# Scores contracted over 128 rows: key parts laid out twice, or padded with zeros

## The chip, the cores and the metric

The kernel runs on one core of a Trainium2 chip. The metric is device time in microseconds (us), the median of several runs. TensorE (PE in the profile) multiplies; its weight loads have a row of their own (PEld). VectorE (DVE), ScalarE (ACT) and GpSimd (POOL) do the rest of the arithmetic, and SyncE (SP) issues most DMAs.

## What is computed

One sequence of 512 tokens with 1024 features goes through two hybrid layers and then one layer of a second kind. Everything is float32. The parts that matter here are the score products; cut to those, the reference is:

```python
# hybrid layer (twice): 6 heads of 64, over 8 chunks of 64 tokens
scores = einsum('bnqhd,bnkhd->bnhqk', q * HEAD_DIM ** -0.5, kb)   # chunk attention, causal by chunk
p = softmax(where(valid, scores + bias, NEG_INF));  o = einsum('bnhqk,bnkhd->bnqhd', p, vb)
q, k = rotary(q), rotary(k) * HEAD_DIM ** -0.5                    # retention
y = (decayed q.k scores within and across chunks) @ v, layer norm, times silu(g)
mix = concat([y_att, y_conv, y_ret]) @ w_out ; then a squared-relu MLP 1024 -> 4096 -> 1024
# second kind: feed-forward, then state space model + dilated attention + attention over a memory, feed-forward
# dilated attention: 3 patterns x 4 heads of 64, windows (128, stride 1), (512, 4), (2048, 16)
```

Every score has a head's 64 dimensions as its contraction.

## The kernel before, in words

Activations lie feature-major: a tile `t` has 128 features in its partitions and the 512 tokens in its columns. So a tile of queries or keys holds two heads, one in rows 0 to 63 and one in rows 64 to 127.

Products keep float32's accuracy by splitting each operand into a high part in TensorE's faster float32r format (by ScalarE, `split`) and the low part that remains (by VectorE, `lo`); three products of parts, high by high, low by high and high by low, are summed in PSUM (`mm3`). All linear layers (`gemm`) do so: weights come by SP as `raw`, are split into `wh` and `wl`, and each 512-token product has 128 rows and 128 columns of weights. They make up nearly all of TensorE's work.

Nothing runs in the order in which it is written. `Plan` records the whole program; `order` then simulates the five engines with a cost for each operation (`_cost`; a matmul's cost there goes by its columns and not by how many rows it contracts) and takes the ready operation of least priority number; `emit` writes the instructions in that order. The order is fixed at build time: each engine, and SP's queue of DMAs, works strictly down its list. `ahead` and `filler` shift priorities. Work beside the linear layers (convolution, attention, retention, state space model) is written as generators that `gemm` steps between its products (`pump_all`, `pump`). All tiles of activations come from one pool of 80 slots (`T`), PSUM has 8 banks (`psa`, `psg`), and weights in flight have 3 `raw` and 4 each of `wh` and `wl`.

The scores:

- Chunk attention and retention (6 heads each, in both hybrid layers) lay the queries of a pair of heads out with `stack`, so that one tile has the high part of a head over its low part, in all 128 rows; `twice` lays the high part of the keys out in both halves. Per block of 128 queries (or keys) there are two products: `mm(qs, kd)` over 128 rows gives high by high plus low by high, and `mm(qs[rows], kl[rows])` over 64 rows gives high by low. Block sizes are 128, 256, 384 and 512 columns. Per layer this is 6 x 4 blocks for each of the two, 96 blocks in both layers. ScalarE and VectorE then read the bank; in retention POOL masks the diagonal (`affine_select`).
- Dilated attention of stride 1 (`dilated_near`, 4 heads x 4 blocks) uses `scores`: three products over 64 rows.
- Dilated attention of strides 4 and 16 (`dilated_far`, 4 heads x 4 residues x 2 patterns) takes plain float32 with one instruction over 64 rows, which the profile counts as two.

`stack` and `twice` move halves between partitions with `move`, a DMA on SP of 64 x 512 elements. The third move of a tile overwrites what the first two have read.

Of the kernel before, what the change touches and what calls it, by code (L numbers as in the profile page):

```python
# [120 lines left out]
def _dilated_bias(table):  # L121
    """per head [128, 256] for the pattern of stride 1 (key block before | same block) and
    [128, 256] for the patterns of strides 4 | 16 within the tokens of one residue modulo 4"""
    t = np.asarray(table, np.float32).reshape(32, 3, DH)
    q = np.arange(P)[:, None]
    k = np.arange(2 * P)[None, :]
    o = q + P - k
    b0 = np.where(((o >= 0) & (o <= P))[..., None], t[_buckets(np.clip(o, 0, P)), 0], np.float32(NEG))
    o = q - np.arange(P)[None, :]
    d = _buckets(4 * np.maximum(o, 0))  # L130
    b1 = np.where((o >= 0)[..., None], t[d, 1], np.float32(NEG))
    b2 = np.where(((o >= 0) & (o % 4 == 0))[..., None], t[d, 2], np.float32(NEG))
    out = np.stack([b0, np.concatenate([b1, b2], axis=1)])
    return np.ascontiguousarray(out.transpose(3, 0, 1, 2), np.float32)


def _pairs(a):
    """[32 groups, 64 states, ...] -> [128 (group % 2, state), 16, ...]"""
    a = np.asarray(a)
    return np.ascontiguousarray(np.moveaxis(a.reshape(PAIRS, 2 * STATE, *a.shape[2:]), 0, 1))  # L140
# [48 lines left out]
class _Engine:  # L189
    """stands for an engine of nc while the program is recorded"""  # L190
# [10 lines left out]
class Plan:  # L201
    """Records the program, orders it by a model of the engines' times (a list scheduler: the ready
    operation of the least priority number goes first) and emits it in that order. An operation that
    takes a slot of a pool ahead of its turn does so only where the operations in between still find
    theirs."""
# [12 lines left out]
    def ahead(self, n):  # L218
        """the operations within count as recorded n operations before"""
        return _Ahead(self, n, False)  # L220

    def filler(self, n):
        """the operations within count as recorded n operations later, and fill gaps before"""
        return _Ahead(self, -n, True)
# [22 lines left out]
    def record(self, eng, fn, method, args, kw):  # L247
# [19 lines left out]
        for w, aps in ((False, reads), (True, writes)):  # L267
            for ap in aps:
# [15 lines left out]
                if n in self.tiles:  # L284
                    t = self.tiles[n]
                    if isinstance(t, str):
                        self.tiles[n] = t = [t, op, op]
                    t[2] = op
                    a = self.acc.setdefault(n, [])
                    if a and a[-1] is not op:  # L290
                        # what opens a tile goes first, and products into a bank keep their order:
                        # the start of one clears the marks of what the others have written there
                        op.deps.add(a[-1] if w and eng == "PE" else t[1])
                    if not a or a[-1] is not op:
                        a.append(op)
# [44 lines left out]
    def order(self):  # L340
# [39 lines left out]
        while len(out) < len(ops):  # L380
# [49 lines left out]
            else:  # L430
# [4 lines left out]
                if e == "PE":  # L435
                    # the clock is halved after a tick of little work
                    tick = int(s / self.TICK)
                    if work.get(tick - 1, 0.0) < 3060:
                        c *= 2
                    work[tick] = work.get(tick, 0.0) + o.cols  # L440
# [53 lines left out]
class Net:  # L494
# [66 lines left out]
    def lo(self, src, hi, out=None):  # L561
        """src - hi as the low part"""
# [12 lines left out]
    def stack(self, src):  # L575
        """parts of two heads -> the high part over the low part of the first, and the low over the high
        part of the second"""
# [8 lines left out]
    def twice(self, src):  # L586
        """parts of two heads -> the high part of each in both halves; the low parts"""
        h, l = src
        o = self.T(F32R)
        lo, hi = slice(0, HD), slice(HD, P)  # L590
        self.move(o[hi], h[hi])
        self.move(o[lo], h[hi])
        self.move(h[hi], h[lo])
        return h, o, l

    def wload(self, src, n=KT * P):
        """one unit of weights, split"""
# [16 lines left out]
    def pump_all(self, bg):  # L614
        """of each [generator, n] in bg n steps"""
# [23 lines left out]
    def gemm(self, srcs, acts, evict, wide=4, bg=None, steps=0, per=1, both=False):  # L639
        """for each source of weights `per` psum tiles [128, S]; the contraction runs outermost  # L640
        over the first `wide` of them"""
# [25 lines left out]
    def rsqrt(self, v, n):  # L667
        """1 / sqrt(v), one step of Newton behind the square root of the table"""
# [10 lines left out]
    def colsum(self, ps, i, m, tile_, rhs, w=1, n=NB):  # L679
        """adds tile_^T rhs to ps[128 tokens, n * w], tile i of m"""  # L680
# [5 lines left out]
    def bcast(self, r, ps=None, n=NB):  # L686
        """r [128 tokens, n] -> psum [128, n * 128], the same in every row"""
# [6 lines left out]
    def bcast2(self, r2):  # L694
        """r2 [128 tokens, NB * 2] -> psum [128, S], rows 0-63 from the first, 64-127 from the second"""
# [14 lines left out]
    def rms_r(self, tiles, n=D, out=True):  # L710
        """1 / rms per token, broadcast to [128, S] in SBUF, or PSUM"""
# [27 lines left out]
    def hsplit(self, x, gname):  # L739
        """x * g per feature, split; the factor per token comes behind the product"""  # L740
        return [self.hsplit1(t, self.col(gname, k)) for k, t in enumerate(x)]

    def post(self, f, gname, nname):
        """x += rms_norm(f) * g; the new x for the norm that follows, as by hsplit"""
# [10 lines left out]
    def vtok(self, vt, b):  # L755
        """tiles [128 features, S] -> psum [128 tokens of block b, heads, 64]"""
# [5 lines left out]
    def vsplit(self, blocks):  # L762
        """token-major values of the blocks of keys, [128 tokens, heads, 64] each -> for block j and
        head h the high part beside the low part, v(j, h) [128, 2, 64]"""
# [21 lines left out]
    def av1(self, v, o, ph, pl, start, stop):  # L786
        """o[0:64] + o[64:128] += v^T probs"""
# [13 lines left out]
    def chunk_attention(self, l, q, k, v, mix):  # L801
        nc = self.nc
        mm = nc.tensor.matmul
        vt = self.vsplit(self.vtok(v, b) for b in range(NB))
        yield
        for h in range(HEADS):
            rows = slice((h % 2) * HD, (h % 2) * HD + HD)
            qs, kd, kl = q[h // 2][h % 2], k[h // 2][h % 2], k[h // 2][2]
# [7 lines left out]
            for b in range(NB):  # L816
# [3 lines left out]
                mm(ps[:, :n], qs[:, c], kd[:, :n], start=True, stop=False)  # L820
                mm(ps[:, :n], qs[rows, c], kl[rows, :n], start=False, stop=True)
# [27 lines left out]
    def fold(self, po, out):  # L849
        """rows 0-63 plus rows 64-127"""  # L850
# [36 lines left out]
    def rotate(self, ps, cr, sr):  # L887
        """the halves of each head trade places by way of DMA"""
# [23 lines left out]
    def retention(self, q, k, v, g, mix):  # L912
        nc = self.nc
        mm = nc.tensor.matmul
        for h in range(HEADS):
            rows = slice((h % 2) * HD, (h % 2) * HD + HD)
            qs, kd, kl = q[h // 2][h % 2], k[h // 2][h % 2], k[h // 2][2]
# [3 lines left out]
            for j in range(NB):  # L921
# [3 lines left out]
                mm(ps[:, :n], kd[:, c], qs[:, j * P:], start=True, stop=False)  # L925
                mm(ps[:, :n], kl[rows, c], qs[rows, j * P:], start=False, stop=True)
# [150 lines left out]
    def exp(self, x, n):  # L1077
        """e^x in place on [128, n], to float32's accuracy"""
# [20 lines left out]
    def cmul(self, ore, oim, are, aim, bre, bim, t, u):  # L1099
        """(ore, oim) = a b; t, u: room"""  # L1100
# [8 lines left out]
    def ssm_prepare(self):  # L1109
        """what depends on the state space model's parameters alone. A chunk of 8 tokens, rows  # L1110
        (7 - token, input) of a group: kernel within the chunk, map to the states at its end, map
        from the states before it, and the states' rotation over the chunks"""
# [183 lines left out]
    def ssm_start(self, tiles):  # L1296
        """tiles of u [128 features, (token of the chunk, chunk)] -> DRAM"""
# [6 lines left out]
    def halves(self, src):  # L1304
        """[P, 1024] of DRAM as two tiles"""
# [5 lines left out]
    def ssm(self, out):  # L1311
        """few columns a product: float32 as it is costs less than its parts"""
# [81 lines left out]
    def softmax_rows(self, s, ps, bias, m, l):  # L1394
        """s = exp(ps + bias - max), the maximum to m, the sum to l"""
# [18 lines left out]
    def vkeep(self, blocks):  # L1414
        """token-major values of the blocks, v(j, h) [128, 64]"""
# [12 lines left out]
    def dilated_near(self, q, k, v, stat, ys):  # L1428
        """stride 1: keys 0 to 128 back"""
# [4 lines left out]
        for h in range(DH):  # L1434
            rows = slice((h % 2) * HD, (h % 2) * HD + HD)
            qq, kk = q[h // 2], k[h // 2]
# [5 lines left out]
            for blocks in ((1, 2), (0, 3)):  # L1442
                ps, s = self.psa(), T()
                c = 0
                for b in blocks:
                    n = 2 * P if b else P
                    self.scores(ps[:, c:c + n], qq, slice(b * P, (b + 1) * P), kk,
                                slice((b + 1) * P - n, (b + 1) * P), rows)
# [29 lines left out]
    def dilated_far(self, q, k, v, stat, ys):  # L1478
        """strides 4 and 16, within the tokens of one residue modulo 4; float32 as it is"""
# [4 lines left out]
        for h in range(DH):  # L1484
# [6 lines left out]
            for r2 in range(2):  # L1491
                ps, s = self.psa(), T(F32, (P, 2, 2, P))
                pv = ps.rearrange("p (r i c) -> p r i c", r=2, i=2)
                for j in range(2):
                    c = slice((r2 * 2 + j) * P, (r2 * 2 + j + 1) * P)
                    for i in range(2):
                        mm(pv[:, j, i], q[i][h // 2][rows, c], k[i][h // 2][rows, c], start=True, stop=True,
                           skip_group_check=True)
# [20 lines left out]
    def dilated_join(self, near, far, y0, y1, out):  # L1519
        """the two parts' sums, each with its own maximum, as one softmax"""  # L1520
# [35 lines left out]
    def memory_start(self):  # L1556
        """the memory, normed but for the factor per token, split"""
# [43 lines left out]
    def memory(self, u):  # L1601
        """keys (u < 4) or values of a head -> DRAM: [128 dims, memory], values [128 memory, dims]"""
# [95 lines left out]
    def tail(self, srcs, acts, out):  # L1698
        """the last products, and behind them the last norm, by halves of the tokens"""
# [73 lines left out]
    def mixer2(self):  # L1773
# [28 lines left out]
        def qkv(pattern, st):  # L1802
            def e(i, ps):
# [10 lines left out]
                st[kind].append(t if kind == 0 or pattern else self.split(t))  # L1814
# [118 lines left out]
```

## Time and profile before

| | |
|---|---|
| three runs | 2509.88, 2514.57 and 2519.38 us, median 2514.57 us |
| profiled execution | span 2510.5 us, 30038 instructions; no further time of its own is given |
| PE busy | 2483.7 us, 99% of the span, 11522 matmuls |
| PEld busy | 2033.4 us (81%) |
| DVE busy | 1462.8 us (58%) |
| ACT busy | 946.0 us (38%) |
| POOL busy | 110.7 us (4%) |
| mean granted TensorE clock | 0.989 of full speed |

The span runs from the first to the last instruction of the profiled execution. Busy time is the union of an engine's instructions; matmuls overlap one another and their ends are modelled, so a busy PE may still be slow. Since every recorded operation is issued from the one line in `emit`, all rows say L475, and they are told apart by their tiles (`t`, `p` for PSUM, `wh`, `wl`) and by their form: `64*128 64x512` is a product over 64 rows with 128 weight columns and 512 columns of output, `128*128 128x512` one over 128 rows. An entry x2 on the timeline is two neighbours of one line and one pair of tiles, merged; the form shown is that of the first. The hybrid layers' mixers lie at about 20 to 230 us and 640 to 870 us, the second kind's mixer at about 1690 to 2030 us.

### The profile page before, as it was taken

To read this page: it belongs to the slowest core of one execution; us is meant where nothing else is said; L and a number is where in the kernel's file an instruction comes from. 1 tells how busy PE (TensorE), PEld (TensorE's weight loads), DVE (VectorE), ACT (ScalarE), POOL (GpSimd) and SP (SyncE) were. 2 spreads that over 40 slices of the span, in tenths; PEclk is the share of its full clock that TensorE was granted. 3 is DMA by queue.
4 is the path that set the end of the run, shared out by engine and by line. 5 is a ranking of instruction groups with operands and counts; after the bars stand their busy time and mean duration, and the time that the engine had idled before them with its cause. 6 is when DMAs were issued, how large, how long until landed. Compare 5 with 4: busy or idle time off the path is not lost.

```text
span 2510.5 us, 30038 instructions
## 1 busy us (share of the span) xinstructions
PE 2483.7 (99%) x11522; PEld 2033.4 (81%) x11522; DVE 1462.8 (58%) x2529; ACT 946.0 (38%) x1482; POOL 110.7 (4%) x214
## 2 busy tenths in 40 slices
PE   8999999999999999999999999999999999999998
PEld 7777888888887788788888888888878888888887
DVE  7985734545897579934565444456445555444445
ACT  4465532223346453322343222234455433322222
POOL 0011000000001100310000000000000000000000
PEclk9998999999999899999999999999999999999999
DMA  6441333233354234533313332265222243232232
GB/s 208 133 124 51 120 109 101 93 101 118 126 143 109 66 120 129 154 119 97 117 61 113 95 106 88 89 225 169 83 77 73 72 137 109 84 109 87 91 107 69
DMA packets 98160, 274.83 MB, mean 109 GB/s; under 512 B 13153, under 2 KB 20001, under 8 KB 98017
## 3 DMA queue, kind: packets, MB, share of 16 engines
q1 hardware_dynamic: 93184, 259.51, 33.1%
q0 software_dynamic: 4832, 13.41, 1.8%
q8 instruction: 90, 1.47, 0.2%
q14 instruction: 54, 0.43, 0.1%
HBM read 242.44 MB, written 19.94 MB: 105 GB/s over the span
## 4 chain that ended last, share of the span: by engine, by line
PE 95%; DVE 3%; ACT 1%; issue 1%; DMA 0%; POOL 0%; DVEq 0%; SPq 0%; ACTq 0%
PE p L475 95%; DVE t L475 2%; ACT t L475 1%; DVE wl L475 0%; ACT wh L475 0%; DMA raw<-in_mem_kv 0%; DVE s L475 0%; POOL t L475 0%; DMA t<-in_x 0%; ACT L475 0%; ACT s L475 0%; DVEq L1929 0%; SPq L475 0%; DVEq L475 0%; ACTq L475 0%
## 5 line engine op out<-in xcount | busy, mean ns | idle before, releaser
L475 PE MATMUL p<-t,wh 128*128 128x512 f32 (+1 forms) x6408 | 1994.4, 390 | 8.2 <-ACT wh L475 7.6
L475 PEld LDWEIGHTS p<-t,wh 128*128 128x128 f32 x6408 | 1201.8, 188 | 259.5 <-ACT wh L475 9.3
L475 PE MATMUL p<-t,wl 128*128 128x512 f32 x3204 | 1248.6, 390 | 1.2 <-DVE wl L475 1.1
L475 ACT ACTIVATE wh<-raw 128x1024 fp32r<-128x1024 f32 (+4 forms) x428 | 426.1, 1000 | 1203.4 <-PE p L475 802.1
L475 PEld LDWEIGHTS p<-t,wl 128*128 128x128 f32 x3204 | 603.3, 188 | 125.4 <-DVE wl L475 3.6
L475 DVE TENSOR_TENSOR wl<-raw,wh 128x1024 fp32r<-128x1024 f32 (+4 forms) x428 | 489.3, 1147 | 144.2 <-ACT wh L475 140.0
L475 DVE TENSOR_TENSOR t<-p,t 128x512 f32<-128x512 f32 (+5 forms) x388 | 238.4, 630 | 488.8 <-PE p L475 463.4
L475 DVE TENSOR_TENSOR t<-t 128x512 f32<-128x512 f32 (+10 forms) x688 | 360.0, 551 | 39.8 <-ACT t L475 32.3
L475 ACT ACTIVATE t<-t 128x512 f32<-128x512 f32 (+4 forms) x405 | 244.6, 617 | 124.9 <-DVE t L475 110.7
L475 PE MATMUL p<-t 128*128 128x256 f32 (+14 forms) x1200 | 233.8, 324 | 5.7 <-DVE t L475 3.6
L475 PEld LDWEIGHTS p<-t 128*128 128x128 f32 (+3 forms) x1200 | 165.5, 179 | 68.5 <-issue 28.6
L475 DVE TENSOR_TENSOR t<-t,p 128x512 f32<-128x512 f32 x104 | 71.7, 692 | 178.3 <-PE p L475 174.0
L475 ACT ACTIVATE t<-p 128x512 f32<-128x512 f32 (+7 forms) x290 | 130.2, 491 | 118.7 <-PE p L475 108.5
L475 DVE SCALAR_TENSOR_TENSOR t<-t,cols 128x512 fp32r<-128x512 f32 (+32 forms) x196 | 132.9, 712 | 4.3 <-ACT t L475 4.2
L475 DVE SCALAR_TENSOR_TENSOR t<-p,t 128x512 f32<-128x512 f32 (+1 forms) x84 | 57.4, 684 | 122.9 <-PE p L475 122.8
L475 ACT ACTIVATE t<-t,cols 128x512 fp32r<-128x512 f32 (+2 forms) x76 | 49.5, 671 | 29.4 <-DVE t L475 28.7
L475 PE MATMUL p<-ident,t 128*128 128x128 f32 x388 | 55.8, 281 | 1.3 <-DVE t L475 1.3
L475 ACT ACT_TABLE_LOAD x41 | 52.6, 1283 | 6.2 <-DMA t<-in_x 4.0
L475 PEld LDWEIGHTS p<-ident,t 128*128 128x128 f32 x388 | 46.9, 144 | 8.7 <-DVE t L475 1.7
L475 ACT ACTIVATE t<-t,s 128x256 f32<-128x256 f32 (+2 forms) x80 | 42.4, 531 | 19.6 <-DVE s L475 18.9
L475 DVE SCALAR_TENSOR_TENSOR t<-t 128x512 f32<-128x512 f32 (+1 forms) x72 | 45.0, 631 | 1.5
L475 DVE CUSTOM_DVE_ANT_0 t<-p,t 128x256 f32<-128x256 f32 (+2 forms) x80 | 34.5, 451 | 13.5 <-PE p L475 13.4
(57 smaller groups left out, 359.7 us busy)
## 6 DMA issues: line engine op xcount, KB each, us to landing
raw<-in_w_in SPq DMA_DIRECT2D x100, 512.0 KB, 3.7
raw<-in_f_in SPq DMA_DIRECT2D x88, 512.0 KB, 3.5
raw<-in_w_up SPq DMA_DIRECT2D x64, 512.0 KB, 3.5
raw<-in_w_down SPq DMA_DIRECT2D x64, 512.0 KB, 3.6
raw<-in_w_out SPq DMA_DIRECT2D x24, 512.0 KB, 3.6
raw<-in_f_down SPq DMA_DIRECT2D x32, 384.0 KB, 3.0
raw<-in_f_down SPq DMA_DIRECT2D x32, 320.0 KB, 2.8
t<-t SPq DMA_DIRECT2D x72, 128.0 KB, 2.3
```

The source lines that it names most:

```text
L475: fn(*args, **kw)
```

## The change

`twice` now lays both parts of the keys out, the high and the low, each in two tiles (one for each head, the head's 64 rows in both halves). `score2` makes two products over 128 rows: the stacked queries by the high keys, and the stacked queries by the low keys. The second also adds the product of the low parts, which was left out before. Stride-1 attention takes the same way (queries through `stack`, keys through `twice`), so that it has two products a block where it had three. For strides 4 and 16 `apart` makes two tiles of a pair of heads' keys, each with the other head's rows set to zero, and the queries' whole tile is used. The rest of the diff removes comments and docstrings.

```diff
     def twice(self, src):
-        h, l = src
-        o = self.T(F32R)
         lo, hi = slice(0, HD), slice(HD, P)
-        self.move(o[hi], h[hi])
-        self.move(o[lo], h[hi])
-        self.move(h[hi], h[lo])
-        return h, o, l
+        out = []
+        for t in src:
+            o = self.T(F32R)
+            self.move(o[hi], t[hi])
+            self.move(o[lo], t[hi])
+            self.move(t[hi], t[lo])
+            out.append((t, o))
+        return list(zip(*out))
+
+    def apart(self, t):
+        lo, hi = slice(0, HD), slice(HD, P)
+        o = self.T()
+        self.nc.gpsimd.memset(o[lo], 0.0)
+        self.nc.scalar.activation(o[hi], t[hi], AF.Copy)
+        self.nc.gpsimd.memset(t[hi], 0.0)
+        return t, o
+
+    def score2(self, o, a, ac, b, bc):
+        mm = self.nc.tensor.matmul
+        for i, (x, y) in enumerate(zip(a, b)):
+            mm(o, x[:, ac], y[:, bc], start=(i == 0), stop=(i == 1), skip_group_check=True)
...
# chunk_attention (retention likewise, with keys and queries exchanged)
-                mm(ps[:, :n], qs[:, c], kd[:, :n], start=True, stop=False)
-                mm(ps[:, :n], qs[rows, c], kl[rows, :n], start=False, stop=True)
+                self.score2(ps[:, :n], (qs, qs), c, kd, slice(0, n))
...
# dilated_near
-                    self.scores(ps[:, c:c + n], qq, slice(b * P, (b + 1) * P), kk,
-                                slice((b + 1) * P - n, (b + 1) * P), rows)
+                    self.score2(ps[:, c:c + n], (qs, qs), slice(b * P, (b + 1) * P), kd,
+                                slice((b + 1) * P - n, (b + 1) * P))
...
# dilated_far
-                        mm(pv[:, j, i], q[i][h // 2][rows, c], k[i][h // 2][rows, c], start=True, stop=True,
+                        mm(pv[:, j, i], q[i][h // 2][:, c], k[i][h // 2][h % 2][:, c], start=True, stop=True,
...
# mixer2, the eviction of queries and keys
-                st[kind].append(t if kind == 0 or pattern else self.split(t))
+                if kind == 1:
+                    st[kind].append(self.apart(t) if pattern else self.twice(self.split(t)))
+                else:
+                    st[kind].append(t if kind == 0 or pattern else self.stack(self.split(t)))
```

## Rows read from the trace of the kernel before

**Rows 1.** The page: busy time per engine, and the chain that ended last.
```profile
PE 2483.7 (99%) x11522; PEld 2033.4 (81%) x11522; DVE 1462.8 (58%) x2529; ACT 946.0 (38%) x1482; POOL 110.7 (4%) x214
...
PE 95%; DVE 3%; ACT 1%; issue 1%; DMA 0%; POOL 0%; DVEq 0%; SPq 0%; ACTq 0%
```

**Rows 2.** Waits of PE: total us, times, longest.
```profile
PE p L475 <- ACT wh L475: 7.6, 1, 7.6
PE p L475 <- DVE t L475: 5.6, 9, 1.7
PE p L475 <- DVE s L475: 2.4, 4, 1.6
PE p L475 <- ACT t L475: 1.8, 5, 0.6
PE p L475 <- DVE wl L475: 1.1, 2, 0.6
PE p L475 <- POOL t L475: 0.9, 2, 0.4
```

**Rows 3.** PE groups by form: products over 64 rows; count, busy us, mean ns, idle before.
```profile
L475 PE MATMUL p<-t 64*128 64x128 f32 x100 | 19.7, 299 | 0.4 <-ACT t L475 0.4
L475 PE MATMUL p<-t 64*128 64x256 f32 x60 | 17.2, 358 | 0.0
...
L475 PE MATMUL p<-t 64*128 64x512 f32 x24 | 13.1, 545 | 0.0
L475 PE MATMUL p<-t 64*128 64x384 f32 x24 | 11.9, 496 | 0.0
```

**Rows 4.** Timeline of PE in a linear layer: start, us, instruction, count.
```profile
82.05 0.62 PE L475 MATMUL p<-t,wh 128*128 128x512 f32 x2
...
82.50 0.39 PE L475 MATMUL p<-t,wl 128*128 128x512 f32 x1
...
82.73 0.62 PE L475 MATMUL p<-t,wh 128*128 128x512 f32 x2
```

**Rows 5.** Timeline of PE at the end of a head's chunk attention scores.
```profile
96.96 0.93 PE L475 MATMUL p<-t 128*128 128x512 f32 x2
...
97.81 0.50 PE L475 MATMUL p<-t,wh 128*128 128x512 f32 x1
```

**Rows 6.** Timeline of PE at two stretches of scores in the first mixer.
```profile
166.73 5.44 PE L475 MATMUL p<-t 128*128 128x128 f32 x16
172.51 0.62 PE L475 MATMUL p<-t,wh 128*128 128x512 f32 x1 [0.34 <-DVE s L475]
172.92 0.63 PE L475 MATMUL p<-t,wl 128*128 128x512 f32 x1
173.35 1.05 PE L475 MATMUL p<-t,wh 128*128 128x512 f32 x2
...
189.06 15.53 PE L475 MATMUL p<-t 128*128 128x128 f32 x34
```

**Rows 7.** The same, closer: two products of 512 columns within the second stretch.
```profile
199.62 1.52 PE L475 MATMUL p<-t 128*128 128x512 f32 x2
...
200.35 1.52 PE L475 MATMUL p<-t 64*128 64x512 f32 x2
```

**Rows 8.** Timeline of PE: stride-1 scores, and strides 4 and 16.
```profile
1768.19 0.90 PE L475 MATMUL p<-t 64*128 64x256 f32 x6
...
1858.92 1.16 PE L475 MATMUL p<-t 64*128 64x128 f32 x8
```

**Rows 9.** Stretches: PE, PEld, DVE, ACT, POOL busy us (instructions), PEclk, DMA share, GB/s.
```profile
30.00:100.00 70.00, 70.00 (x310) 56.82 (x309) 66.28 (x105) 25.79 (x38) 0.40 (x1) 1.00 0.53 151
90.00:212.00 122.00, 120.43 (x531) 89.90 (x530) 93.27 (x225) 73.58 (x157) 16.69 (x30) 0.92 0.36 105
715.00:858.00 143.00, 140.59 (x613) 103.41 (x611) 105.46 (x255) 85.61 (x181) 22.60 (x53) 0.89 0.37 109
1760.00:1870.00 110.00, 109.62 (x606) 88.99 (x605) 44.60 (x126) 49.54 (x117) 3.34 (x5) 1.00 0.26 81
```

**Rows 10.** Waits of SP's DMA queue (us, times, longest), and DMA issues (size, us to landing).
```profile
SPq L475 <- DVE wl L475: 1799.2, 389, 30.1
...
SPq L475 <- DMA t<-t: 33.0, 15, 4.3
...
t<-t SPq DMA_DIRECT2D x72, 128.0 KB, 2.3
```

**Rows 11.** ScalarE and POOL groups by form: a 64-row copy, and a memset.
```profile
L475 ACT ACTIVATE t<-p 64x512 f32<-64x512 f32 x32 | 19.0, 594 | 39.6 <-PE p L475 39.4
...
masks.py:197 POOL MEMSET ident<- 128x128 f32 x1 | 0.2, 204 | 0.3 <-POOLq L1921 0.3
```

More of the change, by code (lines that the diff above doesn't have):

```diff
@@ L802, in chunk_attention @@
         nc = self.nc
-        mm = nc.tensor.matmul
         vt = self.vsplit(self.vtok(v, b) for b in range(NB))
@@ L807, in chunk_attention @@
             rows = slice((h % 2) * HD, (h % 2) * HD + HD)
-            qs, kd, kl = q[h // 2][h % 2], k[h // 2][h % 2], k[h // 2][2]
+            qs, kd = q[h // 2][h % 2], k[h // 2][h % 2]
             if h % 2 == 0:
@@ L913, in retention @@
         nc = self.nc
-        mm = nc.tensor.matmul
         for h in range(HEADS):
             rows = slice((h % 2) * HD, (h % 2) * HD + HD)
-            qs, kd, kl = q[h // 2][h % 2], k[h // 2][h % 2], k[h // 2][2]
+            qs, kd = q[h // 2][h % 2], k[h // 2][h % 2]
             if h % 2 == 0:
@@ L924, in retention @@
                 ps = self.psa()
-                mm(ps[:, :n], kd[:, c], qs[:, j * P:], start=True, stop=False)
-                mm(ps[:, :n], kl[rows, c], qs[rows, j * P:], start=False, stop=True)
+                self.score2(ps[:, :n], kd, c, (qs, qs), slice(j * P, S))
                 nc.scalar.activation(phs[NB - j], ps[:, :n], AF.Copy)
@@ L1435, in dilated_near @@
             rows = slice((h % 2) * HD, (h % 2) * HD + HD)
-            qq, kk = q[h // 2], k[h // 2]
+            qs, kd = q[h // 2][h % 2], k[h // 2][h % 2]
             if h % 2 == 0:
```

## The prediction

> **What bounds the kernel now.** I read the page first. PE is busy 99% of the span and makes 95% of the chain that ended last [rows 1]. PE's waits sum to 19.4 us, of which 7.6 us is the start [rows 2], so 11.8 us of waiting is spread over all the rest. The kernel is as long as PE's list of products, and a change counts by what it does to that list's pace. The other engines count only where they would become late.
>
> So I looked next at what the touched products cost. The groups by form show 208 products over 64 rows [rows 3]: 24 each of 512, 384 and 256 columns and 24 of 128 (the 96 second products of chunk attention and retention), 36 of 256 and 12 of 128 (stride 1), and 64 of 128 (strides 4 and 16, 32 instructions counted as two). Their mean of 299 to 545 ns says little, since records overlap. The pace, from start to start on the timeline, says more. In a linear layer three products of 512 columns start within 82.73 - 82.05 = 0.68 us, 0.227 us each [rows 4]. At the end of a head's attention scores two products of 512 columns, the first over 128 rows and the second over 64, take 97.81 - 96.96 = 0.85 us and not 0.45 [rows 5]. The first is an ordinary product in every way but that the one before it went over 64 rows. So the 0.40 us belongs to the two changes between 128 and 64 rows: 0.20 us each.
>
> A long stretch confirms it. Sixteen products, eight blocks of retention, take 5.44 us [rows 6]. They have 320 columns on average, 0.142 us at the pace of a linear layer, 2.3 us together; the remaining 3.2 us over sixteen changes is again 0.20 us. Where the granted clock is half, two products of 512 columns start 0.73 us apart [rows 7] and those of a linear layer 173.35 - 172.92 = 0.43 us [rows 6], so a change costs 0.30 us there.
>
> **The change part by part.**
>
> *Block 1's scores, over 128 rows.* 96 blocks with two changes each: 192 x 0.20 = 38.4 us, 19.2 us a layer. The columns stay as they are.
>
> *Strides 1, 4 and 16.* The 48 products of stride 1 run in groups of at most six and the 64 of the others in groups of eight [rows 8], so at least 8 + 8 groups, two changes each: 32 x 0.20 = 6.4 us. Dropping one product of three in 16 blocks of 224 columns on average saves 16 x 0.10 = 1.6 us. Plain float32 over 128 rows has no clean row. I take the same price as over 64; at worst its 64 passes take twice their 1.16 / 8 = 0.145 us, 9 us more. A gain has no reason, since the columns are the same.
>
> The Trainium skill speaks against widening: "TensorE: Matmul & The Clock Gate", Part 3 (Packing small matmuls — row/col tiling), says that products over few rows run side by side if they sit in different row groups. Here the rows give no sign of it: six products of 256 columns take 0.90 us, 0.15 us each [rows 8], above the 0.11 us that their columns need. By the rule, with all 208 products (49,664 columns, 22 us at a linear layer's pace) in pairs, the change would give up 11 us and the sum below would be 33 us. A head's products all sit in the same half of the rows, so I don't follow it.
>
> *The clock.* It is 0.92 in the first mixer's scores and 0.89 in the second's [rows 9]. That is 0.08 x 122 = 9.8 us and 0.11 x 143 = 15.7 us of lost time, 25.5 us in all, with nothing lost at strides 1 to 16. PE was not idle before it fell: the first fall shows directly behind the sixteen products of rows 6, and the second within the thirty-four that begin at 189.06. If those runs get dense the clock may hold (25.5 us); if PE waits in them instead, it may fall just as often (0), or more than now (-10 us, as much as the first mixer loses now). I take half, 12.7 us: the runs lose half their length, but the waits below partly replace it.
>
> *VectorE behind the faster PE.* In 90 to 212 us DVE is busy for 93.27 us [rows 9]. Less 19.2 and half of 9.8, the stretch would be 97.9 us, and DVE would be at 95%. That is just what it reaches in 30 to 100 us (66.28 of 70 us) while PE never waits. In the second mixer 105.46 of 143 - 19.2 - 7.9 = 115.9 us is 91%. At strides 1 to 16 (44.60 of 110 us) there is ample room. So in the mixers DVE's slack is used up, and its fixed order will make PE wait now and then. Bounds: nothing, to all that the mixers gain (38.4 + 12.7 = 51 us). I take 12 us, nearest to the waits that PE has now outside the start: as much again. This includes what a new order brings: the order's model of the clock counts a product's rows, so lists shift everywhere, while its price of a product does not know the switch and so does not change.
>
> *More moves on SP.* `twice` issues three moves more for each of 12 pairs in block 1, 36; stride 1 gets 2 x 3 for queries and 2 x 6 for keys, 18. So 54 on top of 72, of 128 KB and 2.3 us to landing each [rows 10]. Each third move waits until the two before it have landed (now 15 such waits, 33.0 us, 2.2 us each), and there are 18 more of them. What stands behind such a wait on SP is the next `raw` of weights, then ACT's and DVE's splits, then PE. The cover: SP stands 1799.2 us waiting for a `raw` buffer to come free, so the weights are far ahead nearly everywhere, and no DMA is among PE's waits [rows 2]. Bounds: nothing, to 54 x 2.3 = 124 us if every landing were waited for by PE. I take 3 us, close to nothing, as the 72 moves of now cost PE nothing that shows.
>
> *apart.* Four copies on ACT of 0.594 us [rows 11], with ACT at 45% there [rows 9], and eight memsets on POOL of 64 x 512: at least the 0.2 us of 128 columns, at most four times that. POOL is busy 3% of the time. Behind a memset on POOL stand only the state space model's DMAs. Linear layers cover all this, and I take nothing; uncovered it would be four chains of 0.6 + 2 x 0.8 us, 9 us.
>
> Sum: 38.4 + 6.4 + 1.6 + 12.7 - 12 - 3 = 44.1 us. The profiled execution's span of 2510.5 us would become 2466.4 us; the page gives no time around the span, and the median of the runs lies 4.1 us above it, so the time would be 2514.6 - 44.1 = 2470 us. What is late next is DVE in the two mixers; elsewhere PE remains the bound.
>
> **The rivals.**
>
> *The clock holds and nothing waits:* 38.4 + 6.4 + 1.6 + 25.5 = 71.9 us, 2443 us. For it: the falls follow only runs of scores. Against it: DVE's 95%.
>
> *VectorE becomes the mixers' bound:* PE's saved time turns into waits there, and the clock stays low. Half of the mixers' 51 us lost, with the moves' 3 us: 2514.6 - 25.6 - 8 + 3 = 2484 us; all of it lost: 2510 us. For it: rows 9. Against it: the stretches have DVE work from the convolution that can be done at any time.
>
> *The 0.20 us isn't the rows' doing* (the change of the operands' tile, say): then nothing goes but one product of three, and 3 us of moves come, 2516 us. Against it: within strides 1 to 16 tiles change too, and six products over 64 rows run at 0.15 us.
>
> *Slower: the moves hold the weights up.* SP's list gets 54 landings more, in the stretches where weights are loaded between moves. If PE waits for a share of their 124 us, the gain of 46.4 us is gone from a share of 37% on, and from 48% it is slower by over 0.5%; at 55% it is 2536 us. For it: the third moves block a queue that works in order. Against it: SP's 1799.2 us of spare waiting.
>
> **How the numbers follow.** Forecast (2452 to 2486 us): 0.60. Clock holds: 0.13. VectorE bound (2486 to 2510 us): 0.17. Not the rows: 0.05. Moves: 0.05. The time is the forecast's, 2470 us. The range of 2442 to 2500 us takes in the full clock below and most of the VectorE case above, and leaves out the last two. Faster by over 0.5% (12.6 us, about what a measurement of this kernel can tell from no change) is the forecast, the full clock and 0.14 of the VectorE case: 0.87; within 0.5% the rest of that and 0.04 of the fourth: 0.07; slower 0.06.
>
> **What would show it.** In the changed profile no form `64*128` is left, and products of 512 columns in the scores start 0.23 us apart; if they still start 0.43 us apart, the 0.20 us was not the rows'. PE's waits on DVE's and ACT's `t` in the mixers show the fifth term, and PEclk there the fourth. Waits of PE or ACT on `raw` or `wh` would show the moves. The prediction is wrong if the mixers' stretches shrink by less than 15 us each.

## The result and the profile after

| | before | changed |
|---|---|---|
| median (lowest to highest) | 2512.23 us (2508.88 to 2519.38) | 2479.22 us (2477.74 to 2481.6) |
| ratio | | 0.9869, 95% interval 0.985 to 0.9888 |
| profiled execution | span 2510.5 us, clock 0.989 | span 2476.0 us, clock 0.994 |

The change makes the kernel 33 us faster (1.3%); 44 us were forecast, and the range of 2442 to 2500 us holds the time. In a later set of runs the same kernel took 2480.62 us, a ratio of 0.9875 (0.986 to 0.989).

The page of the changed kernel, busy time and chain; they answer to [rows 1]:

```profile
PE 2433.8 (98%) x11506; PEld 2018.1 (82%) x11506; DVE 1462.8 (59%) x2529; ACT 946.9 (38%) x1487; POOL 116.9 (5%) x222
...
PE 92%; DVE 3%; ACT 2%; DMA 1%; issue 1%; POOL 0%; SPq 0%; DVEq 0%; ACTq 0%; POOLq 0%
```

PE has 16 products fewer and is busy for 49.9 us less, while the span is 34.5 us shorter: 15 us of the difference came back as waiting. No product over 64 rows is left. The timeline of PE at a head's attention scores, the place of [rows 5]:

```profile
95.44 0.39 PE L475 MATMUL p<-t,wh 128*128 128x512 f32 x1
95.66 1.44 PE L475 MATMUL p<-t 128*128 128x128 f32 x8
96.93 0.40 PE L475 MATMUL p<-t,wh 128*128 128x512 f32 x1
```

Four blocks, eight products of 320 columns on average, start within 96.93 - 95.66 = 1.27 us, 0.16 us each, where sixteen took 5.44 us before [rows 6]: 0.34 us each. A linear layer's pace would be 0.142 us.

PE's waits in the changed kernel (total us, times, longest), as in [rows 2]:

```profile
PE p L475 <- DVE t L475: 15.3, 17, 6.7
PE p L475 <- ACT wh L475: 7.6, 1, 7.6
PE p L475 <- DVE s L475: 6.0, 6, 1.8
PE p L475 <- ACT t L475: 3.7, 5, 1.2
PE p L475 <- DVE wl L475: 1.1, 2, 0.6
PE p L475 <- POOL t L475: 0.9, 2, 0.4
```

They sum to 34.6 us, 15.2 us more than before, and 6.7 us of it is a single wait. The stretches between the same products as in [rows 9] (columns as there):

```profile
30.00:100.00 70.00, 70.00 (x317) 57.84 (x316) 65.82 (x105) 25.38 (x37) 0.88 (x1) 1.00 0.61 166
90.00:193.00 103.00, 97.93 (x521) 80.92 (x518) 92.02 (x221) 69.88 (x151) 16.61 (x30) 1.00 0.51 141
696.00:820.00 124.00, 115.73 (x614) 94.76 (x613) 104.76 (x257) 86.20 (x182) 24.99 (x53) 0.97 0.48 133
1731.00:1836.00 105.00, 103.93 (x595) 86.81 (x595) 44.08 (x127) 51.26 (x120) 4.34 (x7) 1.00 0.27 85
```

The mixers' stretches shrink from 122 to 103 us and from 143 to 124 us. Their clock is back at 1.00 and 0.97, and PE's time without work grew from 1.6 to 5.1 us and from 2.4 to 8.3 us.

Where the single long wait stands is seen on PE's timeline, at the state space model's products:

```profile
1713.03 0.61 PE L475 MATMUL p<-t,wh 128*128 128x512 f32 x2
1720.31 6.66 PE L475 MATMUL p<-t 128*128 128x64 f32 x30 [6.66 <-DVE t L475]
1726.73 0.77 PE L475 MATMUL p<-t,wl 128*128 128x512 f32 x1
1727.30 1.05 PE L475 MATMUL p<-t,wh 128*128 128x512 f32 x2
```

PE stands still for 6.66 us, and a pair of linear products behind it takes 1.05 us and not 0.62 us: half the clock. VectorE (the third engine in the row below), for which PE waits there, is busy for 7.94 of the 8 us before the thirty products:

```profile
1712.00:1720.00 8.00, 1.65 (x8) 1.03 (x6) 7.94 (x11) 1.11 (x2) 0.55 (x2) 0.79 0.30 87
```

In the kernel before, the same thirty products were divided, with products of a linear layer between them, and had the full clock:

```profile
1751.03 0.66 PE L475 MATMUL p<-t 128*128 128x64 f32 x4 [1.74 <-DVE t L475]
...
1753.67 3.01 PE L475 MATMUL p<-t 128*128 128x64 f32 x26
```

To see where each kernel gains, I compare the start of the same product in two traces: there are 3164 products of 128x512 with low weights, always in the same sequence. The starts in the kernel before are 77.7, 677.0, 893.0, 1736.4, 1769.4 and 1901.8 us. The first mixer lies between the first two, the second between the second and the third, the state space model's stalled products between the fourth and the fifth, and the dilated attention between the last two; elsewhere nearly nothing changes. One trace per kernel; in us against the kernel before, minus is faster. The two traces of the changed kernel, whose lists are the same, differ by 1.7, 0.6, 2.3 and 0.0 us in the four columns, so smaller differences in the same column tell nothing:

| kernel | first mixer | second mixer | state space products | dilated attention | median us | ratio, 95% interval |
|---|---|---|---|---|---|---|
| changed | -19.4 | -19.2 | +9.0 | -5.4 | 2479.22 | 0.9869, 0.985 to 0.9888 |
| changed, again (e13) | -17.7 | -18.6 | +11.3 | -5.4 | 2480.62 | 0.9875, 0.986 to 0.989 |
| e1 old order, 128 rows | -16.5 | -26.5 | +1.3 | -4.8 | 2465.87 | 0.9816, 0.9801 to 0.9831 |
| e2 new order, 64 rows | -0.6 | -2.9 | +8.1 | +1.3 | 2518.76 | 1.0029, 1.0017 to 1.0041 |
| e3 hybrid layers only | -16.6 | -24.2 | 0.0 | 0.0 | 2476.04 | 0.9862, 0.9842 to 0.9882 |
| e5 narrow convolution | -16.8 | -17.7 | +6.1 | -5.4 | 2479.53 | 0.9868, 0.9848 to 0.9889 |
| e6 hybrid and stride 1 | -16.8 | -24.1 | +6.4 | -3.4 | 2478.08 | 0.9868, 0.9848 to 0.9887 |
| e7 hybrid and strides 4, 16 | -17.8 | -18.3 | +1.6 | -2.1 | 2477.31 | 0.9862, 0.9847 to 0.9877 |
| e8 scan's price | -16.8 | -18.5 | +8.5 | -5.0 | 2480.28 | 0.987, 0.9854 to 0.9886 |
| e9 products later | -16.2 | -18.2 | +4.6 | -6.1 | 2476.34 | 0.9855, 0.9836 to 0.9874 |
| e10 copy first | -16.3 | -22.3 | +9.5 | -5.3 | 2476.61 | 0.986, 0.9842 to 0.9879 |
| e11 copy first, products later | -16.8 | -21.6 | +4.1 | -6.0 | 2471.84 | 0.9838, 0.9823 to 0.9853 |
| e12 hybrid, 4, 16, copy first | -16.7 | -21.5 | +2.6 | -2.2 | 2474.31 | 0.9849, 0.9834 to 0.9864 |

### The profile page after: what moved, and what is told of

Its sections match the earlier page's. It is cut to its first block, busy times and chain, and to the rows that moved or that the text cites. A ratio compares the mean times of both kernels' runs of the same rounds, so it can differ in the third digit from the quotient of the medians.

```text
span 2476.0 us, 30141 instructions
## 1 busy us (share of the span) xinstructions
PE 2433.8 (98%) x11506; PEld 2018.1 (82%) x11506; DVE 1462.8 (59%) x2529; ACT 946.9 (38%) x1487; POOL 116.9 (5%) x222
## 4 chain that ended last, share of the span: by engine, by line
PE 92%; DVE 3%; ACT 2%; DMA 1%; issue 1%; POOL 0%; SPq 0%; DVEq 0%; ACTq 0%; POOLq 0%
PE p L475 92%; DVE t L475 3%; ACT t L475 1%; DVE wl L475 0%; DMA t<-t 0%; ACT wh L475 0%; DMA t<-sM 0%; POOL t L475 0%; DMA raw<-in_w_in 0%; DVE s L475 0%; DMA raw<-in_w_out 0%; DMA raw<-in_mem_kv 0%; SPq L475 0%; DMA t<-in_x 0%; ACT L475 0%
## 5 line engine op out<-in xcount | busy, mean ns | idle before, releaser
L475 DVE TENSOR_TENSOR t<-t 128x512 f32<-128x512 f32 (+9 forms) x688 | 361.1, 552 | 40.8 <-ACT t L475 30.0
L475 ACT ACTIVATE t<-t 128x512 f32<-128x512 f32 (+3 forms) x409 | 246.9, 617 | 136.9 <-DVE t L475 118.1
L475 PE MATMUL p<-t 128*128 128x256 f32 (+10 forms) x1184 | 190.6, 303 | 15.7 <-DVE t L475 13.1
L475 PEld LDWEIGHTS p<-t 128*128 128x128 f32 (+2 forms) x1184 | 153.1, 177 | 46.6 <-DVE t L475 19.3
L475 PEld LDWEIGHTS p<-ident,t 128*128 128x128 f32 x388 | 45.2, 141 | 11.3 <-ACT t L475 3.0
L475 ACT ACTIVATE t<-t,s 128x128 f32<-128x128 f32 (+2 forms) x80 | 42.3, 531 | 15.0 <-DVE s L475 14.3
L475 DVE CUSTOM_DVE_ANT_0 t<-p,t 128x128 f32<-128x128 f32 (+2 forms) x80 | 34.5, 451 | 9.7 <-PE p L475 9.6
```

What stands on the lines that cost most here:

```text
L475: fn(*args, **kw)
```

## The experiments

**Rows or order?** Two kernels hold the order of one and the products of the other. The first keeps every engine's list of the kernel before, with the 64-row products widened in place; that adds the pair's other head into the scores, and nothing is moved. (The line on `cols` keeps the planner's record of a product as it was, so that the order stays.)

```diff
# e1, on the kernel before; scores and dilated_far likewise
-                mm(ps[:, :n], qs[rows, c], kl[rows, :n], start=False, stop=True)
+                mm(ps[:, :n], qs[:, c], kl[:, :n], start=False, stop=True)
+                self.plan.ops[-1].cols /= 2
```

> The kernel before with its order of instructions kept on every engine; only the 64-row score products are issued over all 128 rows of the same tiles (the second head's rows are added in, so the scores are wrong). No moves, no new tiles, none of the stride-1 products dropped. Theory (each change between 64 and 128 rows costs PE 0.20 us): all 64-row forms go, the pace of 512-column score products becomes 0.23 us, the clock holds mostly, PE waits in the mixers rise by some 10 to 15 us, and the time is 2455 to 2475 us. Rival (the gain of the change came with the new order, or from the dropped products): 2505 to 2515 us, like before.

Measured: 2465.87 us, 45 us less than the 2511.29 us of the kernel before in that set. No 64-row form is left, and the clock is 0.997. Its waits of PE:

```profile
PE p L475 <- DVE t L475: 9.2, 14, 1.7
PE p L475 <- ACT wh L475: 7.5, 1, 7.5
PE p L475 <- DVE s L475: 4.2, 6, 1.6
PE p L475 <- ACT t L475: 2.0, 6, 0.6
PE p L475 <- DVE wl L475: 1.1, 2, 0.6
PE p L475 <- POOL t L475: 0.9, 2, 0.4
```

They rise by 5.5 us only, less than expected. The second kernel keeps the lists, moves and tiles of the change and goes back to 64 rows where the products are issued:

```diff
# e2, on the changed kernel; dilated_far likewise
     def score2(self, o, a, ac, b, bc, rows):
...
             mm(o, x[:, ac], y[:, bc], start=(i == 0), stop=(i == 1), skip_group_check=True)
+            if i:
+                op = self.plan.ops[-1]
+                op.fn = (op.fn[0], (o, x[rows, ac], y[rows, bc]), op.fn[2])
```

> The changed kernel with its order, moves and tiles kept; only the second product of each score block, and the products of strides 4 and 16, are issued over the head's 64 rows. Theory (the switch between row counts): some 224 changes come back, the clock falls again in the mixers, and the time is 2510 to 2530 us, not better than before. Rival (order or moves): 2475 to 2485 us, as the changed kernel.

Measured: 2518.76 us. So with the lists fixed, the number of rows is worth 1.0029 - 0.9869 (intervals in the table) of 2512 us = 40 us on the new lists, and 45 us on the old ones. Without its rows the change makes the kernel 0.3% slower; most of that is the wait at the state space products (8.1 us in the table). It is not the price of lists, moves and tiles alone: in e2 the products of stride 1 alternate between 128 and 64 rows, so that the trace has 240 changes of row count where the kernel before has 226. PE's weight loads show a part of the rows' cost. Waits of PEld that nothing in the profile explains ("issue"), in the kernel before and then in the changed kernel (34.2 us in e2, 6.0 us in e1):

```profile
PEld p L475 <- issue: 34.3, 141, 0.8
```

```profile
PEld p L475 <- issue: 6.8, 26, 0.7
```

**Which part loses in the second kind's mixer?** e3 takes the dilated attention's part of the change back, e6 only that of strides 4 and 16, e7 only that of stride 1.

```diff
# e3 (e6: the split alone where pattern is 0 stays as changed; e7: apart alone stays)
-                if kind == 1:
-                    st[kind].append(self.apart(t) if pattern else self.twice(self.split(t)))
-                else:
-                    st[kind].append(t if kind == 0 or pattern else self.stack(self.split(t)))
+                st[kind].append(t if kind == 0 or pattern else self.split(t))
```

> The change in the hybrid layers alone; dilated attention as before (64 rows, three products for stride 1). Theory (in the second kind's mixer the change gains 5 us at the switches and loses 9 us and more, because TensorE's list has the state space model's products where VectorE is not ready): the stall and the fall of the clock near 1715 us are gone, and the time is 2470 to 2477 us, a little faster than the whole change. Rival (dilated attention gains its 8 us on its own, and the stall is there in any case): 2484 to 2488 us.

Measured: 2476.04 us. The long stall and the fall of the clock are gone (0.0 in the table; the wait there is 1.74 us, as in the kernel before), and the whole change is not faster than its part in the hybrid layers, so dilated attention's gain was used up. The intervals of the two ratios overlap; the table says it, not the medians.

> The change in the hybrid layers and in stride-1 attention; strides 4 and 16 as before (64 rows, no tiles laid apart). Theory (stride 1's part of the change shifts the lists so that PE meets the state space model's products before VectorE has made their inputs): a wait of 5 us or more of PE on VectorE and half the clock behind it near 1715 us, as in the changed kernel; time 2477 to 2484 us. Rival (the copies and memsets of strides 4 and 16 do it): no such wait, 2469 to 2475 us.

> The change in the hybrid layers and at strides 4 and 16; stride 1 as before (three products over 64 rows). Theory (stride 1 shifts the lists): no wait of 5 us near 1715 us, the clock holds there, and strides 4 and 16 gain their 16 switches, 3 us, over the hybrid layers' change alone: 2469 to 2475 us. Rival (the copies and memsets do it): the wait is there, 2477 to 2484 us.

The two at the same place, e6 first:

```profile
1716.31 6.67 PE L475 MATMUL p<-t 128*128 128x64 f32 x30 [4.00 <-DVE t L475]
```

```profile
1715.58 0.66 PE L475 MATMUL p<-t 128*128 128x64 f32 x4 [1.81 <-DVE t L475]
```

With stride 1 changed, the thirty products stand together and wait 4 us (expected: 5 or more); without it they are divided as before and wait 1.81 us. So stride 1's part makes the long wait. It brings two things, though, another list and 18 more moves, and these two kernels don't separate them. The chain that ended last runs, ahead of the thirty products, through DMAs on SP's queue in e6 (a move, a load of weights, an input of the state space model) and through one of them in e7:

```profile
1674.83 8.50 DMA t<-t
1683.39 6.14 DMA raw<-in_w_in
1689.55 5.85 DMA t<-sM
```

```profile
1691.16 5.22 DMA t<-sM
```

The other traces agree: in the kernels without stride 1's moves (before, e1, e3, e7, e12) the chain of the 80 us ahead of the wait has at most 5.94 us of DMAs, and the wait is 1.74 to 2.79 us; in the changed kernel, e13, e2, e5, e6, e8 and e10 it has 13.7 us or more, and the wait is 3.78 to 7.47 us. e7 missed two things that were expected of it: the clock does not hold behind its 1.81 us (0.83 over 1710 to 1720 us), and its time lies above 2475 us. By the medians, 2478.08 and 2477.31 us, the two can't be told apart: e7 loses in the second hybrid mixer, which no theory had expected of a part that comes 900 us later.

**Can the stall be ordered away?**

```diff
# e9, on the changed kernel
-                for g in range(8):
-                    o = ps[:, g * NC:(g + 1) * NC]
+                with self.plan.ahead(-40):
+                  for g in range(8):
+                      o = ps[:, g * NC:(g + 1) * NC]
...
# e8, in _cost
+            if method == "tensor_tensor_scan":
+                n *= 2
```

> The whole change, and the state space model's second group of products recorded 40 operations later, so that products of linear layers stand before and between them. Theory (the stall is a matter of the order of PE's list alone): the wait near 1715 us and the half clock behind it go, dilated attention's gain of 5 to 8 us remains, 2464 to 2470 us, faster than the change. Rival (VectorE's chain for these inputs is what the mixer waits for in any order): a wait of the same length elsewhere in the second kind's mixer, 2476 to 2482 us.

> The whole change, and the planner's price of VectorE's scan doubled, to the 1.2 us that the trace shows for 512 columns. Theory (the lists put PE too early because the planner takes VectorE's chain of scans for shorter than it is): the wait near 1715 us shrinks below 3 us, 2464 to 2472 us. Rival (four scans of 0.6 us too little are not enough to move the products): wait and time as in the changed kernel, 2476 to 2482 us.

Measured: e9 2476.34 us; the longest wait there falls from 6.66 to 2.35 us, but the clock falls behind it all the same, to 0.58 and 0.91 in the two slices of 10 us from 1720 us on, so only half of the loss is gone and the time lies in the rival's range. Stride 1's moves are all there in e9, so the list alone can shorten the wait. e8 2480.28 us: a miss. The planner moved the products, all thirty and the group behind them together, and they wait 3.78 us.

**Does VectorE's load set the mixers' waits?** The prediction's fifth term said so. In e5 the convolution's steps, listed as before, work on 64 columns (the rest of the convolution is left out).

```diff
# e5, on the changed kernel
+                    op = self.plan.ops[-1]
+                    a = acc[i][:, t:t + 64]
+                    op.fn = (op.fn[0], (a, ys[i][:, :64], w, a), op.fn[2])
```

> The changed kernel with its order kept; the convolution's accumulating steps work on 64 of up to 511 columns each (the rest is left out), which takes about 0.55 us off each of 120 VectorE instructions in the two mixers. Theory (in the mixers PE now waits for VectorE's throughput): PE's waits there, some 20 us of gaps, fall by half or more, and the time is 2462 to 2471 us. Rival (PE waits for chains through DMA, ScalarE and VectorE whose length VectorE's load doesn't set): 2475 to 2482 us.

Measured: 2479.53 us, no change. Its stretches, to be read against those of the changed kernel above:

```profile
30.00:100.00 70.00, 70.00 (x317) 57.81 (x316) 45.11 (x96) 24.31 (x33) 2.18 (x2) 1.00 0.60 164
90.00:195.00 105.00, 100.39 (x530) 83.33 (x529) 83.57 (x222) 70.17 (x150) 15.92 (x30) 0.98 0.51 138
698.00:826.00 128.00, 119.50 (x625) 98.63 (x624) 97.32 (x260) 86.45 (x184) 23.61 (x54) 0.96 0.47 130
```

VectorE has 20.7 us less to do before 100 us, and 8.5 and 7.4 us less in the two mixers' stretches, and PE's time without work stays: 4.6 us in the first mixer (5.1 in the change), 8.5 in the second (8.3). So the share of busy time does not set PE's waits: in the first mixer it falls from 92.02 of 103 us (89%) to 83.57 of 105 us (80%). The waits are short and local. At 165 us, for instance, VectorE works without a gap through the retention's values, where no convolution is left, and PE waits 1.63 us there in the change and in e5 alike:

```profile
167.34 0.44 PE L475 MATMUL p<-t 128*128 128x128 f32 x2 [1.63 <-DVE t L475]
```

```profile
168.25 0.44 PE L475 MATMUL p<-t 128*128 128x128 f32 x2 [1.63 <-DVE t L475]
```

What shortening VectorE's list at those places would give was not tried.

**Why does a part at 1700 us cost the second hybrid mixer?** In the table the six kernels with 128 rows and `apart` as written gain 17.7 to 19.2 us there, the three without it 24 us or more. The changed kernel's POOL timeline at the start shows it:

```profile
0.95 0.52 POOL L475 MEMSET t<- 64x512 f32 x1
1.52 0.28 POOL masks.py:199 TENSOR_SCALAR_AFFINE_SELECT ident<-ident 128x128 f32<-128x128 f32 x1
1.76 1.44 POOL L475 MEMSET t<- 64x512 f32 x3
```

`apart` opens its new tile with a memset that depends on nothing. The planner finds four such operations ready at the start and lets the idle POOL do them, and four of the 80 tile slots are held from 1 us to about 1700 us. With the copy ahead of the memset, the tile opens when the keys are there:

```diff
# e10, in apart (e11: with e9's edit; e12: with stride 1 as before)
-        self.nc.gpsimd.memset(o[lo], 0.0)
         self.nc.scalar.activation(o[hi], t[hi], AF.Copy)
+        self.nc.gpsimd.memset(o[lo], 0.0)
```

> The whole change with two lines of apart exchanged: ScalarE's copy opens the new tile and POOL's memset follows, so that the four memsets no longer run in the first 4 us of the kernel and hold four of the 80 tile slots until the second kind's mixer. Theory (the held slots change the hybrid mixers' lists and cost the second one 3 to 6 us): the second mixer gains 22 to 23 us against the kernel before, where the change gains 17 to 19, the stall near 1715 us remains, and the time is 3 to 6 us below that of the change in the same set of runs, 2472 to 2477 us. Rival (slots to spare; the difference seen between kernels with and without apart is the clock's hazard): mixers and time as in the change, 2477 to 2481 us.

> As the kernel with the copy first, and the state space model's second group of products recorded 40 operations later. Theory (both losses are matters of the lists, and add): another 2 to 5 us less, 2468 to 2474 us. Rival (the wait for VectorE's chain only moves, and the clock falls as before): within 2 us of the kernel with the copy first alone.

> The change in the hybrid layers and at strides 4 and 16, with the copy first; stride 1 as before. Theory (held slots, and stride 1 shifting the state space model's products): neither loss, 2469 to 2474 us, with PE's wait near 1715 us under 2.5 us and the second mixer's gain 22 to 23 us. Rival (neither is a matter of these parts): 2476 to 2480 us.

> The changed kernel itself, unchanged, as the reference of this set: 2477 to 2482 us. If it lies within 1 us of the kernel with the copy first, the slots cost nothing that can be measured.

Measured, all in one set: the change 2480.62, e10 2476.61, e11 2471.84, e12 2474.31 us. The second mixer gains 21.5 to 22.3 us in the three and 18.6 us in the change, so the early memsets cost 3 to 4 us there. That it is by the slots which they hold follows from how the planner works; the runs show only what the exchange of two lines does. Some 2 us to the kernels without `apart` stay open. The memsets of e10 now stand where the keys are made:

```profile
1698.45 0.55 POOL L475 MEMSET t<- 64x512 f32 x1
1711.77 1.10 POOL L475 MEMSET t<- 64x512 f32 x2 [12.77 <-issue]
```

By the times alone e10 is not clear of the change (its interval reaches from 0.9842 to 0.9879, that of the change from 0.986 to 0.989). e11 is, with 0.9823 to 0.9853: 8.8 us less than the change, and 40 us less than the kernel before. Of the kernels that compute the scores as the change does, it has the lowest median. e12 came out 0.3 us above its range: its wait near 1715 us is 2.79 us and not under 2.5, and the clock falls there too (0.83 over 1715 to 1725 us). In the old place e11 still waits, and behind it a pair of linear products takes 1.05 us, at half the clock:

```profile
1716.73 0.66 PE L475 MATMUL p<-t 128*128 128x64 f32 x4 [1.89 <-DVE t L475]
...
1726.03 1.05 PE L475 MATMUL p<-t,wh 128*128 128x512 f32 x2
```

## Why the prediction was right, step by step

- **The switch (38.4 + 6.4 us): right in the mechanism.** The pace is close to that of a linear layer, 64-row products alone bring the time back (e2), and widening alone gives the gain on the old lists (e1). The rival that the 0.20 us wasn't the rows' doing falls with e2. One reading that the prediction brought against that rival was wrong: the six products at 1768.19 us [rows 8] are three of 256 and three of 128 columns, and their 0.90 us include a change of rows. The second and the third take 0.118 and 0.112 us from start to start, the pace of a linear layer for 256 columns (0.113 us); the passes of strides 4 and 16 start 0.112 us apart, and not 0.145. So 64-row products among themselves are not slow; the change costs, as the sum had it. The rule in the Trainium skill's "TensorE: Matmul & The Clock Gate", Part 3, by which products over few rows in different row groups run side by side, would have taken 11 us off by the prediction's estimate. No run here tests it, since neighbours over 64 rows always belong to one head and so to the same half of the rows; e1, where only rows were added, is 45 us faster.
- **Strides 1, 4 and 16 (6.4 + 1.6 us): mis-sized.** Dilated attention gained 5.4 us in the change. Stride 1 gave 3.4 us of 4.8 (e6) and strides 4 and 16 gave 2.1 us of 3.2 (e7). In the change 0.7 us more of the stretch pass without work of PE (1.07 of 105 us; 0.38 of 110 us before); what keeps the rest was not settled.
- **The clock (12.7 us): too small in the mixers, and brought near by a loss elsewhere.** By the prediction's measure 25.5 us were lost in the mixers before; by the rows above 0.03 x 124 = 3.7 us are lost after, so 21.8 us came back. The measure itself is too high: where changes of rows stand close, two products start 0.73 us apart at half the clock and 0.43 at full [rows 5, rows 7], so half the clock costs 41% of such a stretch and not half of it. And the clock fell anew behind the stall: 0.83, 0.50 and 0.98 in the three slices of 10 us from 1710 us on, 6.9 us lost, which leaves 14.9 us.
- **Waits (12 us): right in size in the mixers, wrong in reason.** PE's time without work grew by 3.5 and 5.9 us there, 9.4 us. The reason given, VectorE's busy share, does not bear out: 95% was forecast and 89% measured, and in e5 it is 80% with the waits unchanged.
- **No wait priced in the second kind's mixer: the step that cost most.** The "ample room" was read from VectorE's 44.60 of 110 us at strides 1 to 16, and there it held (44.08 of 105 us after). But that stretch begins behind the state space model's products, where VectorE has no room. In the changed kernel thirty products stand before their inputs, and PE waited 6.66 us and then ran at half the clock: 9.0 us in the change, 11.3 us in its second profile. The kernel before met the same products with 1.74 us of waiting. How much of this is the list and how much the DMAs behind stride 1's moves is open. A new order was priced with one sum for the whole kernel, and not place by place.
- **Moves (3 us): not measured by themselves.** No DMA is among PE's own waits, so the rival in which PE waits for a share of 124 us did not come. But the moves are not hidden everywhere: the chain that ended last, which ran through no move before, now runs through them for 3.85 us at 152 us and 5.61 us at 757 us (in e1, with the old moves, for 1.89 and 2.81 us), and stride 1's eighteen stand in SP's queue right ahead of the state space model's inputs, whose wait is the largest loss of all.
- **apart (0 us): wrong by a way that I didn't look at.** Copies and memsets are hidden, as said, but the memsets ran at the start and held four tile slots for 1700 us, and with that the second mixer lost 3 to 4 us.

The two mixers together were forecast at 38.4 + 12.7 - 12 - 3 = 36.1 us and gained 38.6 us. That they agree so well is in part luck: with the clock and the waits as measured, 38.4 + 21.8 - 9.4 = 50.8 us, 12 us more than came. The clock's measure explains at most some 5 us of it (an estimate: 41% and not half of the 51 us that the mixers spent at half the clock before); the rest is open. The shortfall lies in the second kind's mixer: 8.0 us of gain forecast, 3.6 us lost.

## What to carry to other kernels

Where TensorE is the bound, read its pace from start to start between neighbours of different shapes: a product over part of the rows can cost its neighbours as much as itself (0.20 us for each of two changes here, beside 0.227 us for 512 columns), and products with the rows filled, by useful data or zeros, take no longer than their columns. What fills the rows is not free, though: here the moves, tiles and the new list gave some 9 us back at one place. In a program whose order comes from a planner, hold the order fixed and change one thing at the emission, to tell an instruction's own cost from what a reshuffled list does elsewhere. Look for operations without inputs that open a buffer: a planner like this one runs them at once and holds the buffer until its use.

## What was not expected of the hardware

How much a wait costs beyond itself, and that its length does not tell. The 6.66 us before the state space model's products brought half the clock behind them; so did 1.89 us in e11 and 2.35 us in e9, while 1.74 us in the kernel before did not: the clock is 1.00 over 1751 to 1761 us. The list does not tell either. e1 has the list of the kernel before and the same wait of 1.74 us, and behind it the clock falls to 0.50 (1712 to 1714 us). The pairs of linear products behind the wait, in the kernel before and then in e1:

```profile
1751.50 0.71 PE L475 MATMUL p<-t,wh 128*128 128x512 f32 x2
```

```profile
1711.76 1.05 PE L475 MATMUL p<-t,wh 128*128 128x512 f32 x2
```

So a part of what the table shows at these products may be chance; the difference was not settled.

A change in the columns of weights can cost the same as one in rows. In the changed kernel a product of 512 columns between two groups with 64 columns of weights, in dilated attention's plain float32 products, takes 0.43 us from start to start:

```profile
1826.66 0.43 PE L475 MATMUL p<-t 128*64 128x128 f32 x2
1827.02 0.50 PE L475 MATMUL p<-t,wh 128*128 128x512 f32 x1
1827.45 2.83 PE L475 MATMUL p<-t 128*64 128x128 f32 x22
```

In the hybrid mixers, where products with 64 columns of weights are made of parts, neighbours keep the ordinary pace (at 106.46 us one of 512 and one of 384 columns take 0.41 us together). No run separates the two cases, and no kernel here tried to widen these.

And the moves: the same DMA of 128 KB took 2.3 us to land at the median with 72 of them [rows 10], in e1 too, which is 45 us faster, and 4.1 us with 126. The eighteen of stride 1 take 6.2 us (1600 to 1720 us). Over the whole changed kernel:

```profile
t<-t SPq DMA_DIRECT2D x126, 128.0 KB, 4.1
```
